# The memory layer of a two-layer trunk: rows read back through DRAM, one transpose for the sample's sums, a low split issued later, a bias on GpSimd, two PSUM pools exchanged

## The chip, the cores and the metric

The kernel runs on one core of one Trainium2 chip. The metric is the device time of one execution in microseconds; 956.14 us is the median of three runs of the kernel before.

Engines are named as the profile names them: PE (TensorE matmul, with its weight load PEld), DVE (VectorE), ACT (ScalarE), POOL (GpSimd), SP (SyncE, which issues the DMAs).

## The reference

One inference step of a two-layer trunk with 256 prompt tokens and 8 samples of 8 tokens, width 1024. Layer 0 mixes tokens by a gated spatial MLP, layer 1 by an mLSTM matrix memory of 8 heads (keys 128 wide, values 256 wide); a gated MLP with a short convolution follows each. The change lies in the memory layer, whose core is, for each head and chunk:

```python
qk, new_buf = causal_dwconv(qk_pre, conv_buf, conv_w, conv_b)
qk = silu(qk)                                   # q, and k scaled
...
w_intra = jnp.exp(D - m_t[..., None])           # gates, masked
w_inter = jnp.exp(inter - m_t)
sc = einsum('bhtd,bhsd->bhts', qc, kc) * w_intra
num = w_inter * einsum('bhtd,bhde->bhte', qc, C) + einsum('bhts,bhse->bhte', sc, vc)
den = w_inter * einsum('bhtd,bhd->bht', qc, n) + sum(sc)
h = num / maximum(abs(den), exp(-m_t))
...
C_new = decay * C + einsum('bhsd,bhse->bhde', kg, vc)
...
hn = (h - mean(h)) * rsqrt(var(h) + EPS) * gn_g
y = (sigmoid(o_pre) * hn) @ w_out
```

Prompt and samples share the weights, so all 320 tokens go through each projection together, and the samples' memories C are eight inputs and eight outputs per head.

## The kernel before

**Projections.** All weights come from DRAM in the order in which they are used, as pieces of up to 128 x 1024 (`raw`, four buffers, issued by SP four pieces ahead). Each is split for precision into a high part `wh` (a cast on ACT, line 154) and a low part `wl` (a subtraction on DVE, line 155), three buffers each, made one piece ahead. `chunk` then issues 24 matmuls for the 8 k-steps of a piece: `wh` with the high part of the activations, `wh` with their low part, `wl` with the high part. `block` does one output block of 128 x 320 and accumulates it in a bank of the PSUM pool `psm` (three banks, tag `pm`). All else uses the pool `psa` (five banks, tag `pa`). Banks of a pool are given out in turn, so an operation that takes a bank waits for the last reader of what stood in it.

**Order.** The order on PE is the order of the program. The splits are pinned in the program's order too (`hold`). The other instructions of DVE, ACT, POOL and SP are placed by a list scheduler that knows the data dependences and has a cost for each; `issue_after` puts an instruction behind a given one, and `pin` fixes its place among its neighbours.

**Memory layer** (`layer_b`; some 420 to 716 us of the span). `gates` computes the rows of all heads' gates, 8 x 392 (`Xf`), and their two-part form `X`. A loop over the heads h then does, in this order: the projections of `q` and `k`, with convolution and SiLU (`qk_epi`: POOL copies, ACT `bcv` line 765, DVE `bcv` line 767); the attention of head h-1 with its states (`inter`, `numer`), its statistics (`stats`: DVE `t`, POOL `sl` line 953, DVE `nb` line 957, ACT `hn` line 965); the two blocks of `v` (`v_epi`, copied by ACT to `vTb`, lines 785 and 786); the scores (`scores`); the two blocks of the output gate (`o_epi`: DVE `o_b` line 995, ACT `th_o`); `finish` of head h-1 (transposes `phn`, DVE `y_b` line 1009, ACT `yhb`, DVE `ylb` line 1012); the state updates of the samples (`state_sample`: PE `pcs`, DVE `C` line 990, and the store `out_Cs`); and the natural forms of k and v (`k_nat`, `v_nat`: transposes `pk` and `pv`).

- The rows reach all 128 partitions in `scores` by a matmul, `pMb`, with a selector `sel` of 128 x 8 x 128. ACT's `w` (line 805) and DVE's `qw` and `dec` read its bank.
- The normalised sums `hn` are [128, 3, 256]: two thirds for the prompt, the last third for the 64 rows of the samples, padded with zeros. Six 128 x 128 transposes bring them back, three for each half of 256, and each half has its own `y_b` of 320 columns.
- In `o_epi(h, 1, blk())` the gate's second block takes a weight piece and so issues the split of the next one; `finish(h - 1)` follows.
- `early` runs blocks of the output projection ahead, in the heads 5 to 7 (two of them at the end of the head of number 4): they read `yhb`, `ylb` of the heads done.
- Head 7 has no next head: its second gate block comes after `pCp` (`state_prompt`) in the tail, then the rest of the output projection.

Of the kernel before, what the change touches and what calls it, by code (L numbers as in the profile page):

```python
# [37 lines left out]
class Net:  # L38
# [26 lines left out]
    def weights(self):  # L65
# [48 lines left out]
        self.loaded, self.halved, self.used = [], [], 0  # L114

# [4 lines left out]
    def prefetch(self, n, m):  # L120
# [8 lines left out]
        while len(self.halved) < min(m, len(self.wq)):  # L129
# [25 lines left out]
            self.last_low = nc.vector.tensor_tensor(wl[:, :kn, :], raw[:, :kn, :], wh[:, :kn, :].bitcast(F32), op=SUB)  # L155
            self.hold(self.last_low)
            self.halved.append((wh, wl))

# [26 lines left out]
    def block(self, kt, rhs):  # L185

        ps = self.psm.tile([P, 512], F32, tag="pm", name="pm")
# [447 lines left out]
    def layer_b(self):  # L635
# [5 lines left out]
        with ExitStack() as ctx:  # L641
# [6 lines left out]
            sel = lp.tile([P, NH, P], F32R, name="sel")  # L648
# [12 lines left out]
            def gates(rp):  # L661
# [3 lines left out]
                selr = rp.tile([P, NH, P], F32, name="selr")  # L665
# [59 lines left out]
                nc.scalar.activation(Xf[:, T:392], wi, AF.Exp)  # L725
                nc.vector.tensor_copy(X[0:8], Xf)
# [61 lines left out]

            def scores(h):
# [3 lines left out]
                pb = self.psa.tile([P, 512], F32, tag="pa", name="pMb")  # L793
                sc = self.psa.tile([P, 512], F32, tag="pa", name="psc")
                if h:
                    mm(pb[:, :392], sel[:, h, :], X, True, True)
# [3 lines left out]
                if not h:  # L800

                    mm(pb[:, :392], sel[:, h, :], X, True, True)
# [11 lines left out]
                dec = hp.tile([P, NB], F32, tag="dec", name="dec", bufs=2)  # L814
                nc.vector.tensor_copy(dec, pb[:, 384:392])
# [39 lines left out]
            def k_nat(h):  # L855
                s = S[h]
                ks = s["k"][0]
                pk = self.psa.tile([P, 512], F32, tag="pa", name="pk")
# [72 lines left out]
            def stats(h, between=None):  # L931
# [19 lines left out]
                self.t_made = nc.vector.scalar_tensor_tensor(t1, t1, 1e-36, mv[:, :, 1], op0=MAX, op1=ADD)  # L951
                sl = hp.tile([P, 3], F32, tag="sl", name="sl", bufs=1)
                nc.gpsimd.tensor_tensor(sl, t1, self.mhalf.to_broadcast([P, 3]), op=ALU.pow)
                if between:
                    between()
                nb = hp.tile([P, 3], F32, tag="nb", name="nb", bufs=1)
                made = nc.vector.scalar_tensor_tensor(nb, mv[:, :, 0], -1.0, sl, op0=MULT, op1=MULT)
                if between:
                    self.pin(made)
                for t in range(3):  # L960
# [39 lines left out]
            def finish(h):  # L1000
# [3 lines left out]
                for e in range(2):  # L1004
                    pt = self.psa.tile([P, 512], F32, tag="pa", name="phn")
                    for t in range(3):
                        self.tr(pt[:, t * P:(t + 1) * P], hn[:, t, e * P:(e + 1) * P], self.ident)
# [292 lines left out]
```

## Time and profile before

| | |
|---|---|
| median of 3 runs | 956.14 us (955.89 to 956.53) |
| profiled execution | 956.05 us |
| its span | 954.3 us |
| PE clock granted in it | 0.999 |
| busy: PE, PEld, DVE, ACT, POOL | 947.3, 933.8, 697.3, 531.9, 115.8 us |
| DMA | 155.19 MB, 163 GB/s mean |

The profile is one execution on the chip. A row of a timeline gives start, duration (of all instructions in the row, where it ends in x2 and more), engine, line and operation, output and inputs, and in brackets the idle time before it with what ended it. Matmuls are pipelined, so a matmul's cost is read from start to start. A row of stretches gives start:end, the length, and then PE, PEld, DVE, ACT and POOL busy time with instruction counts, the PE clock, the share of the DMA engines and GB/s.

### The profile page before, as it was taken

To read this page: it belongs to the slowest core of one execution; us is meant where nothing else is said; L and a number is where in the kernel's file an instruction comes from. 1 tells how busy PE (TensorE), PEld (TensorE's weight loads), DVE (VectorE), ACT (ScalarE), POOL (GpSimd) and SP (SyncE) were. 2 spreads that over 40 slices of the span, in tenths; PEclk is the share of its full clock that TensorE was granted. 3 is DMA by queue.
4 is the path that set the end of the run, shared out by engine and by line. 5 is a ranking of instruction groups with operands and counts; after the bars stand their busy time and mean duration, and the time that the engine had idled before them with its cause. 6 is when DMAs were issued, how large, how long until landed. Compare 5 with 4: busy or idle time off the path is not lost.

```text
span 954.3 us, 17131 instructions
## 1 busy us (share of the span) xinstructions
PE 947.3 (99%) x6427; PEld 933.8 (98%) x6427; DVE 697.3 (73%) x1331; ACT 531.9 (56%) x978; POOL 115.8 (12%) x291
## 2 busy tenths in 40 slices
PE   9999999999999999999999999999999999999997
PEld 8889999999999999999999999999999999999997
DVE  6766976577777754559999998788897777775443
ACT  7557543454555443458777876666766445544342
POOL 2200000010000000014333322102102000000000
PEclk9999999999999999999999999999999999999999
DMA  8643346444444465565465655553474444445441
GB/s 270 210 153 133 133 137 198 160 146 147 149 156 155 139 183 147 149 216 175 128 212 175 206 178 196 185 183 118 132 247 148 149 145 154 156 144 155 143 141 56
DMA packets 54214, 155.19 MB, mean 163 GB/s; under 512 B 7372, under 2 KB 11980, under 8 KB 54132
## 3 DMA queue, kind: packets, MB, share of 16 engines
q1 hardware_dynamic: 54132, 154.10, 50.5%
q8 instruction: 51, 0.84, 0.4%
q14 instruction: 31, 0.25, 0.1%
HBM read 142.10 MB, written 11.97 MB: 161 GB/s over the span
## 4 chain that ended last, share of the span: by engine, by line
PE 94%; DVE 3%; ACT 1%; POOL 1%; DMA 0%; issue 0%; SPq 0%; POOLq 0%
PE pm L54 81%; PE pv_a L54 6%; PE num L54 2%; PE pmix L54 1%; PE pcs L54 1%; PE psc L54 1%; PE phn L57 0%; PE pCp L54 0%; DMA raw<-in_a_wv 0%; PE pv L57 0%; DVE wl L155 0%; PE pc L54 0%; DVE bcv L767 0%; PE pg L54 0%; PE pk L57 0%
## 5 line engine op out<-in xcount | busy, mean ns | idle before, releaser
L154 ACT CAST wh<-raw 128x1024 fp32r<-128x1024 f32 (+3 forms) x256 | 257.0, 1004 | 294.1 <-PE pm L54 161.7
L155 DVE TENSOR_TENSOR wl<-raw,wh 128x1024 fp32r<-128x1024 f32 (+3 forms) x256 | 299.0, 1169 | 118.9 <-ACT wh L154 115.0
L54 PE MATMUL pm<-xh,wh 128*128 128x320 f32 x1216 | 372.3, 311 | 0.1
L54 PE MATMUL pm<-xl,wh 128*128 128x320 f32 x1216 | 370.3, 309 | 0.0
L54 PE MATMUL pm<-xh,wl 128*128 128x320 f32 x1216 | 321.2, 309 | 0.0
L54 PEld LDWEIGHTS pm<-xh,wh 128*128 128x128 f32 x1216 | 228.4, 188 | 0.4 <-DVE o_b L995 0.3
L54 PEld LDWEIGHTS pm<-xl,wh 128*128 128x128 f32 x1216 | 228.4, 188 | 0.2
L54 PEld LDWEIGHTS pm<-xh,wl 128*128 128x128 f32 x1216 | 214.5, 188 | 0.0
L54 PE MATMUL pm<-yh_f,wh 128*128 128x320 f32 x352 | 108.8, 309 | 0.0
L54 PE MATMUL pm<-yl_f,wh 128*128 128x320 f32 x352 | 108.8, 309 | 0.0
L54 PE MATMUL pm<-yh_f,wl 128*128 128x320 f32 x352 | 108.8, 309 | 0.0
L54 PEld LDWEIGHTS pm<-yh_f,wh 128*128 128x128 f32 x352 | 66.1, 188 | 0.0
L54 PEld LDWEIGHTS pm<-yl_f,wh 128*128 128x128 f32 x352 | 66.1, 188 | 0.0
L54 PEld LDWEIGHTS pm<-yh_f,wl 128*128 128x128 f32 x352 | 66.1, 188 | 0.0
L531 DVE SCALAR_TENSOR_TENSOR fcv<-fpad,vecs,fcv 128x336 f32<-128x336 f32 x88 | 49.6, 565 | 2.1 <-ACT fcv L529 0.7
L54 PE MATMUL pm<-yh_a,wh 128*128 128x320 f32 x128 | 39.6, 310 | 0.0
L54 PE MATMUL pm<-yh_a,wl 128*128 128x320 f32 x128 | 39.5, 309 | 0.0
L54 PE MATMUL pm<-yl_a,wh 128*128 128x320 f32 x128 | 39.5, 309 | 0.0
L533 ACT ACTIVATE fgl<-fcv 128x256 f32<-128x256 f32 x44 | 18.2, 414 | 37.8 <-DVE fcv L531 37.8
L54 PE MATMUL pm<-yhb,wh 128*128 128x320 f32 x128 | 38.1, 311 | 0.0
L54 PE MATMUL pm<-ylb,wh 128*128 128x320 f32 x128 | 37.8, 309 | 0.0
L303 DVE TENSOR_TENSOR xT<-pm,xT 128x320 f32<-128x320 f32 x39 | 19.1, 489 | 25.1 <-PE pm L54 24.9
(286 smaller groups left out, 1371.7 us busy)
## 6 DMA issues: line engine op xcount, KB each, us to landing
raw<-in_f_up SPq DMA_DIRECT2D x88, 512.0 KB, 3.3
raw<-in_b_win SPq DMA_DIRECT2D x48, 512.0 KB, 4.0
raw<-in_f_dn SPq DMA_DIRECT2D x32, 448.0 KB, 3.3
C<-in_C SPq DMA_DIRECT2D x32, 258.0 KB, 3.7
out_Cs<-C SPq DMA_DIRECT2D x32, 258.0 KB, 2.5
raw<-in_a_win SPq DMA_DIRECT2D x16, 512.0 KB, 3.3
raw<-in_a_wo SPq DMA_DIRECT2D x16, 512.0 KB, 4.3
raw<-in_f_dn SPq DMA_DIRECT2D x16, 512.0 KB, 3.5
```

The costliest lines, as they stand in the source:

```text
L54: self.pin(self.nc.tensor.matmul(out, lhsT, rhs, start=start, stop=stop, skip_group_check=skip))
L154: self.last_split = self.hold(nc.scalar.copy(wh[:, :kn, :], raw[:, :kn, :]))
L155: self.last_low = nc.vector.tensor_tensor(wl[:, :kn, :], raw[:, :kn, :], wh[:, :kn, :].bitcast(F32), op=SUB)
L303: self.nc.vector.tensor_tensor(x, ps[:, :T], x, op=ADD)
L531: nc.vector.scalar_tensor_tensor(cv, pd[:, i:i + NC], self.vec(w + i * KF), cv, op0=MULT, op1=ADD)
L533: nc.scalar.activation(gl[:, :TP], cv[:, :TP], AF.Gelu_apprx_tanh)
```

## The change

- `gates` writes the rows `Xf` to a DRAM buffer; for h of 1 and more `rows_in(h)` reads row h back into all partitions (`Mb`, two buffers), and `scores` uses it in place of the `pMb` matmul. Head 0 keeps the matmul. `sel` shrinks to 128 x 128, and `dec` is copied for head 0 alone.
- The samples' normalised sums go to `hs` [128, 128], the two halves of 128 one above the other; one transpose brings them back. `y_b` becomes two instructions over both halves, one for the prompt (2 x 256) and one for the samples (2 x 64).
- For heads 1 to 6 the low split issued by the gate's second block is put off and issued behind the first `y_b` of `finish`.
- `nb` is computed on POOL from a negated mean `nm` (DVE).
- `pk` of `k_nat` takes a bank of `psm` (h < 7); head 7's second gate block takes one of `psa`; a further `prefetch` stands behind `begin(2)`.

The order of matmuls and transposes on PE stays as it was, but for the 7 `pMb` and 8 `phn` that are gone. On the other engines the scheduler makes a new order: on DVE `o_b`, `y_b` (2 x 256), `wl`, `y_b` (2 x 64), two `C`, `kgs`, two `ylb`; on ACT the three `w` of the next head stand before its `bcv`, at the end of the head before; on SP the read of `Mb` stands right behind the store `out_Cs` of the fourth state step, and `rows` is written after `out_m`.

```diff
@@ -112,6 +112,7 @@
         ffn(1)
         self.wq = q
         self.loaded, self.halved, self.used = [], [], 0
+        self.late, self.put_off = [], False
 
     AHEAD, SPLIT_AHEAD = 4, 1
     low_last = False
@@ -152,9 +153,16 @@
                 self.halved.append((wh, wl))
                 continue
             self.last_split = self.hold(nc.scalar.copy(wh[:, :kn, :], raw[:, :kn, :]))
-            self.last_low = nc.vector.tensor_tensor(wl[:, :kn, :], raw[:, :kn, :], wh[:, :kn, :].bitcast(F32), op=SUB)
-            self.hold(self.last_low)
             self.halved.append((wh, wl))
+            self.late.append((wl[:, :kn, :], raw[:, :kn, :], wh[:, :kn, :]))
+            if not self.put_off:
+                self.low_parts()
+
+    def low_parts(self):
+
+        for wl, raw, wh in self.late:
+            self.last_low = self.hold(self.nc.vector.tensor_tensor(wl, raw, wh.bitcast(F32), op=SUB))
+        self.late = []
 
     @contextmanager
     def behind_split(self):
@@ -182,9 +190,10 @@
                 if sweep:
                     self.mm(ps[:, :T], wl[:, k, :], xh, False, last and k == kn - 1)
 
-    def block(self, kt, rhs):
-
-        ps = self.psm.tile([P, 512], F32, tag="pm", name="pm")
+    def block(self, kt, rhs, ps=None):
+
+        if ps is None:
+            ps = self.psm.tile([P, 512], F32, tag="pm", name="pm")
         done = 0
         while done < kt:
             kn = self.wq[self.used][3]
@@ -645,7 +654,7 @@
             gnh = lp.tile([P, 16], F32, name="gnh")
             colsT = lp.tile([P, 3, 96], F32, name="cols")
             X = lp.tile([P, 392], F32R, name="X")
-            sel = lp.tile([P, NH, P], F32R, name="sel")
+            sel = lp.tile([P, P], F32R, name="sel")
             mk = lp.tile([P, NB], F32, name="mk")
             mo = lp.tile([8, 9], F32, name="mo")
             pads = []
@@ -662,7 +671,7 @@
 
                 bif = rp.tile([40, 1 + NB], F32, name="bif")
                 rst = rp.tile([40, 2, T], F32, name="rst")
-                selr = rp.tile([P, NH, P], F32, name="selr")
+                selr = rp.tile([P, P], F32, name="selr")
                 RS = rp.tile([P, 384], F32, name="RS")
                 nc.sync.dma_start(bif, I["b_if"])
                 nc.sync.dma_start(rst, I["seg"])
@@ -723,6 +732,8 @@
                 nc.vector.tensor_tensor(seg(wi[:, :64]), m0.unsqueeze(2).to_broadcast([8, NB, NS]), seg(M[:, TP:]), op=SUB)
                 nc.vector.tensor_tensor(wi[:, 64:72], m0, ML, op=SUB)
                 nc.scalar.activation(Xf[:, T:392], wi, AF.Exp)
+
+                nc.sync.dma_start(I["rows"], Xf)
                 nc.vector.tensor_copy(X[0:8], Xf)
                 nc.vector.tensor_tensor(X[32:40], Xf, X[0:8].bitcast(F32), op=SUB)
                 nc.vector.tensor_scalar(gnh, self.vecs[:, V_GN:V_GN + 16], 0.5, None, op0=MULT)
@@ -786,20 +797,23 @@
                 nc.scalar.copy(vT[:, T:384], ps[:, TP:T])
                 S[h].setdefault("vT", []).append(vT)
 
+            def rows_in(h):
+                mb = hp.tile([P, 392], F32, tag="Mb", name="Mb", bufs=2)
+                nc.sync.dma_start(mb, I["rows"][h:h + 1, :].to_broadcast([P, 392]))
+                S[h]["rows"] = mb
+
             def scores(h):
                 s = S[h]
                 q, qh, ql = s["q"]
                 k, kh, kl = s["k"]
-                pb = self.psa.tile([P, 512], F32, tag="pa", name="pMb")
+                pb = s["rows"] if h else self.psa.tile([P, 512], F32, tag="pa", name="pMb")
                 sc = self.psa.tile([P, 512], F32, tag="pa", name="psc")
-                if h:
-                    mm(pb[:, :392], sel[:, h, :], X, True, True)
                 mm3(sc[:, :TP], kh, kl, qh, ql, True, True)
                 mm(sc[:, TP:384], k[:, P:TP], q[:, P:TP], True, True)
                 mm(sc[:, 384:448], k[:, TP:384], q[:, TP:T], True, True)
                 if not h:
 
-                    mm(pb[:, :392], sel[:, h, :], X, True, True)
+                    mm(pb[:, :392], sel, X, True, True)
                 w = hp.tile([P, 448], F32, tag="w", name="w", bufs=1)
                 for (n, o, c0, c1, t) in ((P, 0, 0, TP, 0), (P, TP, P, TP, 1), (64, 384, TP, T, 2)):
                     nc.scalar.activation(w[:n, o:o + c1 - c0], pb[:n, c0:c1], AF.Exp, scale=-1.0, bias=colsT[:n, t, h:h + 1])
@@ -811,8 +825,10 @@
                                         channel_multiplier=1)
                 nc.gpsimd.affine_select(w3, w3, pattern=[[NS, NB], [1, NS]], compare_op=ALU.is_ge, fill=0.0, base=0,
                                         channel_multiplier=-1)
-                dec = hp.tile([P, NB], F32, tag="dec", name="dec", bufs=2)
-                nc.vector.tensor_copy(dec, pb[:, 384:392])
+                dec = pb[:, 384:392]
+                if not h:
+                    dec = hp.tile([P, NB], F32, name="dec")
+                    nc.vector.tensor_copy(dec, pb[:, 384:392])
                 qw = hp.tile([P, 64], F32, tag="qw", name="qw", bufs=1)
                 nc.vector.scalar_tensor_tensor(qw, q[:, TP:T], 0.5, pb[:, T:384], op0=MULT, op1=MULT)
                 Qd = Qz.rearrange("p (b e) -> p b e", e=136)
@@ -855,7 +871,8 @@
             def k_nat(h):
                 s = S[h]
                 ks = s["k"][0]
-                pk = self.psa.tile([P, 512], F32, tag="pa", name="pk")
+                pool, tag = (self.psm, "pm") if h < NH - 1 else (self.psa, "pa")
+                pk = pool.tile([P, 512], F32, tag=tag, name="pk")
                 for t in range(3):
                     self.tr(pk[:, t * P:(t + 1) * P], ks[:, t * P:(t + 1) * P], self.ident)
                 kgh = hp.tile([P, 2, P], F32R, tag="kgh", name="kgh", bufs=1)
@@ -949,20 +966,27 @@
                 t1 = hp.tile([P, 3], F32, tag="t1", name="t1", bufs=1)
                 nc.vector.scalar_tensor_tensor(t1, rd, EPS, rd, op0=MULT, op1=MULT)
                 self.t_made = nc.vector.scalar_tensor_tensor(t1, t1, 1e-36, mv[:, :, 1], op0=MAX, op1=ADD)
+                nm = hp.tile([P, 3], F32, tag="nm", name="nm", bufs=1)
+                nc.vector.tensor_scalar(nm, mv[:, :, 0], -1.0, None, op0=MULT)
                 sl = hp.tile([P, 3], F32, tag="sl", name="sl", bufs=1)
                 nc.gpsimd.tensor_tensor(sl, t1, self.mhalf.to_broadcast([P, 3]), op=ALU.pow)
+                nb = hp.tile([P, 3], F32, tag="nb", name="nb", bufs=1)
+                nc.gpsimd.tensor_tensor(nb, nm, sl, op=MULT)
                 if between:
                     between()
-                nb = hp.tile([P, 3], F32, tag="nb", name="nb", bufs=1)
-                made = nc.vector.scalar_tensor_tensor(nb, mv[:, :, 0], -1.0, sl, op0=MULT, op1=MULT)
-                if between:
-                    self.pin(made)
-                for t in range(3):
-                    n = P if t < 2 else 64
-                    if h == NH - 1 and t:
-                        nc.vector.tensor_scalar(hn[:n, t, :], src[t][:n, :DV], mv[:n, t, 0:1], sl[:n, t:t + 1], op0=SUB, op1=MULT)
+                last = h == NH - 1
+                for t in range(2):
+                    if last and t:
+                        nc.vector.tensor_scalar(hn[:, t, :], src[t][:, :DV], mv[:, t, 0:1], sl[:, t:t + 1], op0=SUB, op1=MULT)
                     else:
-                        nc.scalar.activation(hn[:n, t, :], src[t][:n, :DV], AF.Identity, scale=sl[:n, t:t + 1], bias=nb[:n, t:t + 1])
+                        nc.scalar.activation(hn[:, t, :], src[t][:, :DV], AF.Identity, scale=sl[:, t:t + 1], bias=nb[:, t:t + 1])
+
+                for e in range(2):
+                    a, z = hs[64 * e:64 * e + 64, :], ns[:, e * P:(e + 1) * P]
+                    if last:
+                        nc.vector.tensor_scalar(a, z, mv[:64, 2, 0:1], sl[:64, 2:3], op0=SUB, op1=MULT)
+                    else:
+                        nc.scalar.activation(a, z, AF.Identity, scale=sl[:64, 2:3], bias=nb[:64, 2:3])
 
             def state_prompt(h):
                 s = S[h]
@@ -993,20 +1017,29 @@
             def o_epi(h, j, ps):
                 o = lp.tile([P, T], F32, tag="ob", name="o_b", bufs=1)
                 nc.vector.tensor_tensor(o, ps[:, :T], self.rb, op=MULT)
-                th = lp.tile([P, T], F32, tag="tho", name="th_o", bufs=4)
-                nc.scalar.activation(th, o, AF.Tanh, scale=0.5)
-                S[h].setdefault("o", []).append(th)
+                if not j:
+                    S[h]["o"] = lp.tile([P, 2, T], F32, tag="tho", name="th_o", bufs=2)
+                nc.scalar.activation(S[h]["o"][:, j, :], o, AF.Tanh, scale=0.5)
 
             def finish(h):
                 s = S[h]
                 yh = hp.tile([P, 2, T], F32R, tag="yhb", name="yhb", bufs=6)
                 yl = hp.tile([P, 2, T], F32R, tag="ylb", name="ylb", bufs=6)
+                pt, ps = [self.psa.tile([P, 512], F32, tag="pa", name="phn") for _ in range(2)]
                 for e in range(2):
-                    pt = self.psa.tile([P, 512], F32, tag="pa", name="phn")
-                    for t in range(3):
-                        self.tr(pt[:, t * P:(t + 1) * P], hn[:, t, e * P:(e + 1) * P], self.ident)
-                    y = self.tp.tile([P, T], F32, tag="yf", name="y_b", bufs=2)
-                    nc.vector.scalar_tensor_tensor(y, s["o"][e], 1.0, pt[:, :T], op0=ADD, op1=MULT)
+                    for t in range(2):
+                        self.tr(pt[:, (2 * e + t) * P:(2 * e + t + 1) * P], hn[:, t, e * P:(e + 1) * P], self.ident)
+                self.tr(ps[:, :P], hs, self.ident)
+                yb = lp.tile([P, 2, T], F32, name="y_b", bufs=1)
+                o = s["o"]
+                for c, n, x in ((slice(0, TP), TP, pt), (slice(TP, T), 64, ps)):
+                    made = nc.vector.scalar_tensor_tensor(yb[:, :, c], o[:, :, c], 1.0, x[:, :2 * n].rearrange("p (e t) -> p e t", e=2), op0=ADD, op1=MULT)
+                    if self.put_off:
+                        self.put_off = False
+                        with tc.issue_after(made.ins):
+                            self.low_parts()
+                for e in range(2):
+                    y = yb[:, e, :]
                     g = gnh[:, 2 * h + e:2 * h + e + 1]
                     nc.scalar.activation(yh[:, e, :], y, AF.Copy, scale=g)
                     nc.vector.scalar_tensor_tensor(yl[:, e, :], y, g, yh[:, e, :].bitcast(F32), op0=MULT, op1=SUB)
@@ -1025,8 +1058,8 @@
             vb = hp.tile([P, CW], F32R, name="vb")
             Qz = hp.tile([P, 8 * 136], F32R, name="Qz")
             Ps = hp.tile([P, P], F32R, name="Ps")
-            hn = hp.tile([P, 3, DV], F32, name="hn")
-            nc.gpsimd.memset(hn[64:, 2, :], 0.0)
+            hn = hp.tile([P, 2, DV], F32, name="hn")
+            hs = hp.tile([P, P], F32, name="hs")
             nc.gpsimd.memset(vh[:, :, DV:DV + 1].bitcast(F32), 1.0)
             nc.gpsimd.memset(vh[:, :, DV + 1:].bitcast(F32), 0.0)
             nc.gpsimd.memset(vl[:, :, DV:].bitcast(F32), 0.0)
@@ -1056,6 +1089,7 @@
 
             for h in range(NH):
                 if h:
+                    rows_in(h)
                     qk_epi(h, 0, blk())
                     early(h, 0)
                     if h == 1:
@@ -1099,8 +1133,8 @@
                     for i in (0, 1):
                         state_split(h, i)
                 if h and not last:
+                    self.put_off = True
                     o_epi(h, 1, blk())
-                if h and not last:
                     finish(h - 1)
                     state_sample(h - 1, 3)
                 k_nat(h)
@@ -1133,10 +1167,11 @@
             v_first(h)
             state_prompt(h)
             k_mask(h)
-            o_epi(h, 1, blk())
+            o_epi(h, 1, self.block(KD, self.x_rhs, self.psa.tile([P, 512], F32, tag="pa", name="pm")))
             finish(h)
             state_sample(h, 0)
             begin(2)
+            self.prefetch(0, self.used + 2)
             state_sample(h, 1)
             for m in range(KD):
                 ps = part.get(m)
...
@@ -1280,6 +1313,7 @@
     arrays = _lay_out({k: np.asarray(v) for k, v in inputs.items()})
     nc = bacc.Bacc("TRN2", target_bir_lowering=False, num_devices=1)
     I = {k: nc.dram_tensor("in_" + k, v.shape, F32, kind="ExternalInput").ap() for k, v in arrays.items()}
+    I["rows"] = nc.dram_tensor("rows", (NH, 392), F32).ap()
     O = {k: nc.dram_tensor("out_" + k, s, F32, kind="ExternalOutput").ap() for k, s in _OUTS.items()}
     with tile.TileContext(nc) as tc:
         Net(nc, tc, I, O).run()
```

More of the change, by code (lines that the diff above doesn't have):

```diff
@@ L1262, in _lay_out @@
     a["seg"] = seg
-    sel = np.zeros((P, NH, P), f)
-    for h in range(NH):
-        sel[h, h] = 1.0
-        sel[32 + h, h] = 1.0
+    sel = np.zeros((P, P), f)
+    sel[[0, 32]] = 1.0
     a["sel"] = sel
```

## The prediction

> **What bounds the kernel now.** I read the page's busy times and its chain of work first, then what TensorE (PE) waited for, the table of stretches, and the timelines of PE, VectorE (DVE), GpSimd (POOL) and ScalarE (ACT) around the edits.
>
> ```profile
> PE 947.3 (99%) x6427; PEld 933.8 (98%) x6427; DVE 697.3 (73%) x1331; ACT 531.9 (56%) x978; POOL 115.8 (12%) x291
> ...
> PE 94%; DVE 3%; ACT 1%; POOL 1%; DMA 0%; issue 0%; SPq 0%; POOLq 0%
> ```
>
> ```profile
> PE pv L57 <- DVE y_b L1009: 0.6, 1, 0.6
> ```
>
> ```profile
> 449.00:479.00 30.00, 29.23 (x210) 28.56 (x208) 28.68 (x73) 23.96 (x59) 10.87 (x24) 1.00 0.50 149
> ```
>
> PE works through the whole span and its clock is 1.00: a microsecond is won only by issuing less on PE or by closing a gap in it. The one named gap in the memory layer is in head 1 (the stretch from 449 us; the columns after the length are PE, weight load, DVE, ACT, POOL). DVE is busy 28.68 of 30 us there, so whatever is moved on DVE moves something else.
>
> **The change part by part**
>
> *Rows read back.* Seven `pMb` matmuls go (heads 1 to 7).
>
> ```profile
> 467.75 0.34 PE L54 MATMUL pMb<-X,sel 128*128 128x392 f32 x1
> 467.93 0.30 PE L54 MATMUL psc<-qh,kh 128*128 128x256 f32 x1
> ```
>
> From its start to the next start is 0.18 us: 7 x 0.18 = 1.26 us of PE issue, with nothing else put there: **-1.26**. The same rows now come by one DMA of 1.5 KB each way; what they may hold up stands in the last rival.
>
> *One transpose for the sample's sums.* Eight heads issue five transposes instead of six.
>
> ```profile
> 505.65 0.82 PE L57 MATMUL phn<-ident,hn 128*128 128x128 f32 x6
> ...
> 506.88 0.82 PE L57 MATMUL pv<-ident,vTb 128*128 128x128 f32 x6
> 507.45 0.36 PE L54 MATMUL num<-Ch,Qz 128*128 128x258 f32 x1
> ```
>
> Six transposes of this form (`pv`, 506.88 to 507.45) take 0.57 us, so one is 0.095, rounded to 0.10: **-0.8**.
>
> *The split behind the gate's step.* The rows of head 1 on PE and on DVE:
>
> ```profile
> 477.26 0.60 PE L57 MATMUL pv<-ident,vTb 128*128 128x128 f32 x4
> 478.44 0.44 PE L57 MATMUL pv<-ident,vTb 128*128 128x128 f32 x2 [0.58 <-DVE y_b L1009]
> 478.93 0.36 PE L54 MATMUL num<-Ch,Qz 128*128 128x258 f32 x1
> ```
>
> ```profile
> 476.37 1.22 DVE L155 TENSOR_TENSOR wl<-raw,wh 128x1024 fp32r<-128x1024 f32 x1
> 477.51 0.48 DVE L995 TENSOR_TENSOR o_b<-pm,rb 128x320 f32<-128x320 f32 x1
> 477.91 0.87 DVE L1009 SCALAR_TENSOR_TENSOR y_b<-th_o,phn 128x320 f32<-128x320 f32 x2
> ```
>
> From the first `pv` to `num` PE needs 1.67 us here and 0.57 in head 2 (506.88 to 507.45): 1.10 us of waiting for the bank that `y_b` reads, because a low split of 1.14 us (476.37 to 477.51) was put ahead of `o_b`. In the new order the DVE runs `o_b`, the first `y_b`, then the split. What is late next? `num` now needs the bank of that first `y_b`, of 2 x 256. Head 2 gives the start:
>
> ```profile
> 505.92 0.49 DVE L995 TENSOR_TENSOR o_b<-pm,rb 128x320 f32<-128x320 f32 x1 [0.47 <-PE pm L54]
> ```
>
> ```profile
> 472.71 0.56 DVE L824 SCALAR_TENSOR_TENSOR Pf<-psc,w 128x384 f32<-128x384 f32 x1 [0.23 <-POOL w L807]
> ```
>
> `o_b` starts 0.27 after the first transpose (505.65 to 505.92), `y_b` 0.40 later (477.51 to 477.91). The new `y_b` has 512 columns: at least the 0.56 of a 384-column one, at most the 0.87 of the pair; I take 0.65, since it is one instruction. It ends 1.32 after the first transpose (1.23 to 1.54), and `num` is due at 1.80 less one transpose, 1.70. So no wait in any of heads 1 to 6, and the whole **-1.1** is gained.
>
> *The last gate block in the other pool.*
>
> ```profile
> 683.77 0.28 PE L54 MATMUL pCp<-vl,kgh 128*128 128x258 f32 x1
> 683.89 0.28 PE L54 MATMUL pCp<-vh,kgl 128*128 128x258 f32 x1
> 684.22 0.42 PE L54 MATMUL pm<-xh,wh 128*128 128x320 f32 x1
> ```
>
> 0.33 us from the last `pCp` to the gate block, where the `pCp` before it was followed after 0.12: **-0.2**, as it no longer waits for the previous gate's `o_b` to free its bank. `k_nat` in the small pool costs nothing: the bank that its turn there brings was last read by the state update that DVE runs ahead of `o_b`, and `o_b` is done 0.27 + 0.49 us after the first transpose (head 2's rows), `pk` comes after all five.
>
> *What the later split makes late.* The early blocks of the output projection (after heads 4, 5, 6) use both `ylb` and low parts that DVE now makes after the split.
>
> ```profile
> 564.59 1.18 DVE L1012 SCALAR_TENSOR_TENSOR ylb<-y_b,gnh,yhb 128x320 fp32r<-128x320 f32 x2
> ...
> 566.20 0.34 DVE L870 SCALAR_TENSOR_TENSOR kgs<-pk,cols,kgs 32x128 fp32r<-32x128 f32 x1
> ...
> 569.90 2.35 DVE L155 TENSOR_TENSOR wl<-raw,wh 128x1024 fp32r<-128x1024 f32 x2
> ```
>
> ```profile
> 562.72 0.82 PE L57 MATMUL phn<-ident,hn 128*128 128x128 f32 x6
> ...
> 567.28 0.31 PE L54 MATMUL pm<-ylb,wh 128*128 128x320 f32 x1
> ...
> 570.95 1.34 PE L54 MATMUL pm<-yhb,wl 128*128 128x320 f32 x8
> ```
>
> With head 2's steps the new DVE order runs, counted from the first transpose: `o_b` at 0.27, the first `y_b` at 0.67, the split at 1.32 (1.14 long), the second `y_b` (0.15), two state updates (0.4 each, the step from `o_b` to `y_b`), `kgs` (0.34, with its neighbour's overlap 0.3): `ylb` starts at 3.7 and ends at 4.9. Head 4's transposes began at 562.72, so the matmul of 567.28 is due at 4.56, 0.1 earlier without the sixth transpose: **+0.4** (0 to 0.6). The low part read at 570.95, due at 8.2 - 0.1 + 0.4 = 8.5, is now the split behind all that: from `kgs` to the split DVE took 3.70 us (566.20 to 569.90), of which that `kgs` and a residual add, 0.8, fall away; 3.7 + 1.1 for the two `ylb` + 2.9 + 1.2 for the split is 8.9: **+0.4** (0.1 to 0.7). After heads 5 and 6, where more blocks lie between, I put **+0.15** for both.
>
> ```profile
> 695.66 1.22 DVE L155 TENSOR_TENSOR wl<-raw,wh 128x1024 fp32r<-128x1024 f32 x1
> ```
>
> ```profile
> 697.10 1.34 PE L54 MATMUL pm<-yhb,wl 128*128 128x320 f32 x8
> ```
>
> Behind head 7 the low part ends at 696.88, only 0.22 before its matmul. The extra prefetch and the earlier gate block change what stands in front of such a split on DVE by one step of 0.4 to 0.9 (a state update or a residual add): **+0.4** (0 to 0.6).
>
> *Bias by GpSimd.* `nb` leaves DVE, where it waited for POOL's `sl`, and follows it on POOL:
>
> ```profile
> 468.09 0.86 POOL L953 TENSOR_TENSOR sl<-t,mhalf 128x3 f32<-128x3 f32 x1 [0.82 <-DVE t L951]
> ...
> 495.61 1.77 POOL L953 TENSOR_TENSOR sl<-t,mhalf 128x3 f32<-128x3 f32 x1 [2.27 <-DVE t L951]
> ```
>
> ```profile
> 495.45 1.21 DVE L155 TENSOR_TENSOR wl<-raw,wh 128x1024 fp32r<-128x1024 f32 x1
> 497.41 0.16 DVE L957 SCALAR_TENSOR_TENSOR nb<-mv,sl 128x3 f32<-128x3 f32 x1 [0.75 <-POOL sl L953]
> ```
>
> ```profile
> 470.89 0.21 ACT L786 COPY vTb<-pm 128x64 f32<-128x64 f32 x1
> ...
> 499.32 0.21 ACT L786 COPY vTb<-pm 128x64 f32<-128x64 f32 x1
> ```
>
> ```profile
> 472.51 0.31 PE L54 MATMUL pm<-xh,wh 128*128 128x320 f32 x1
> ...
> 502.13 0.31 PE L54 MATMUL pm<-xh,wh 128*128 128x320 f32 x1
> ```
>
> DVE stops standing idle for 0.75 us in head 2, and only a non-critical engine gains by that. Behind `nb` queue the normalisation and the copies `vTb` on ACT, whose end frees the bank of the second gate block: 1.4 us of slack in head 1 (471.10 to 472.51), 2.6 in head 2 (499.53 to 502.13). `nb` on POOL lies between 0.2 us (as `nb` on DVE) and another 1.77; I take 0.5, covered by that slack: **0**.
>
> The sum: -1.26 - 0.8 - 1.1 - 0.2 + 0.4 + 0.4 + 0.15 + 0.4 = **-2.0 us**. The profiled execution took 956.05 us (a span of 954.3 and 1.75 around it), 0.09 below the median of the runs, 956.14. So 954.1 us against the median. About 0.2%, 1.9 us, is what a measurement can tell from no change.
>
> **The Trainium skill on the bias.** Where DVE sits in a two-input split (495.45), `sl` took 1.77 us, where that was not beside it (468.09) 0.86. The Trainium skill, GPSIMD Engine Reference, section "Engine selection", says to keep elementwise arithmetic on VectorE, and section "Specifications" that GpSimd's interfaces to SBUF are shared with VectorE, in contention when it runs with two SBUF inputs. The two rows agree with that, and it speaks against this part. Its price is the second rival.
>
> **The rivals**
>
> *1. The late splits do not bite* (the new waits of 1.35 us are absent): -3.36 us, 952.8 us. For it: each of the four is smaller than one DVE step, and PE needs nothing else new. Against: DVE is the fuller engine here.
>
> *2. The bias is slow.* Both POOL steps stand beside splits, 2 x 1.77 us. In head 1 they end at 468.09 + 3.54 = 471.63 instead of 469.1, 2.5 later, against 1.4 of slack: +1.1. In head 2 they end at 499.15 instead of 497.57, 1.6 later, inside 2.6. Sum -0.9 us: 955.2. Or the late parts cost their upper ends (0.6, 0.7, 0.3, 0.6 instead of 1.35 in all): -1.15, 955.0. Both are no change.
>
> *3. Slower: the rows land late.* The `w` exponentials no longer follow a matmul but a DMA, and stand on ACT at the end of the head before, with casts `wh` and the `bcv` steps of the next `q` queued behind them; on SP the read stands behind the state's store and ahead of weights.
>
> ```profile
> 508.62 0.47 DVE L990 SCALAR_TENSOR_TENSOR C<-C,dec,pcs 128x258 f32<-128x258 f32 x1
> ```
>
> ```profile
> 513.33 0.67 ACT L765 ACTIVATE bcv<-bpad,vecs 128x344 f32<-128x344 f32 x1
> ```
>
> ```profile
> raw<-in_b_win SPq DMA_DIRECT2D x48, 512.0 KB, 4.0
> ...
> out_Cs<-C SPq DMA_DIRECT2D x32, 258.0 KB, 2.5
> ```
>
> The buffer of the rows is free when the state update at 508.62 ends (509.1). At 2.5 to 4.0 us to landing the rows are there at 511.6 to 513.1, ahead of `bcv` at 513.33, and ACT goes on. It decides from a landing of about 6 us: then `bcv`, the conversions behind it and the scores of heads 2 to 7 come 2 us or more later, and their margin is some 2.5. At +0.7 in each of six heads, +4.2 - 2.0 = +2.2: 958.3 us. For it: DMA engines are half busy here (0.50 in the stretch), and it hits every head. Against: no row above lands that late.
>
> **How the numbers follow.** Forecast (953.3 to 954.9, its four waits up or down by half) 0.40; rival 1 0.20; rival 2 in its two forms 0.21; rival 3 0.19. The forecast's own interval straddles the 0.2% bound (954.2): a bit over half of it (0.23), with rival 1 and a little of rival 2 (0.03), gives faster 0.46; the rest of both (0.17 and 0.18) same 0.35; the third rival slower 0.19. The range goes from rival 1 with nothing to spare (952.3) up to four fifths of the third rival's price (957.4), and leaves out about 2 in 10.
>
> **What would show it.** Right: no `pMb` after head 0, five `phn` per head, no wait of PE for `y_b` at head 1, short waits of PE for `ylb` or `wl` after head 4 and behind head 7. Wrong: PE waiting for `psc` operands, or for a copy of `vTb`, in several heads; `w` waiting for a DMA on ACT for microseconds; `sl` with `nb` above 3 us in head 1.

## The result, and the profile after

The changed kernel took 967.50 us (median of 4 runs, 967.42 to 968.83) against 956.03 us before: ratio 1.0122 (95% interval 1.0105 to 1.014), 11.5 us slower. The forecast was 954.1 us, with a range up to 957.4.

The page's busy times and chain of the kernel after:

```profile
PE 947.5 (98%) x6412; PEld 931.9 (97%) x6412; DVE 700.7 (73%) x1325; ACT 535.6 (55%) x985; POOL 123.5 (13%) x298
...
PE 86%; DVE 9%; ACT 2%; issue 1%; DMA 1%; POOL 1%; SPq 0%; DVEq 0%; ACTq 0%
```

What PE waited for, after (total, times, longest):

```profile
PE pm L54 <- DVE wl L164: 7.7, 7, 1.5
PE pcs L54 <- ACT vTb L797: 2.1, 1, 2.1
PE pm L54 <- DVE ylb L1045: 1.0, 2, 0.7
...
PE num L54 <- DVE y_b L1036: 0.8, 3, 0.3
```

The stretch of head 1, after (columns as in the prediction):

```profile
449.00:479.00 30.00, 27.89 (x199) 27.64 (x200) 25.32 (x67) 24.01 (x60) 13.12 (x23) 1.00 0.46 150
```

PE issues 15 instructions fewer and its clock is the same, but 8% of the chain has gone from PE to others. DVE has hardly more work than before (700.7 us against 697.3): it comes late with nearly the same work. In the stretch of head 1 it is even less busy, 25.32 us against 28.68. The gap that the change aimed at (`pv` waiting for `y_b`) is gone, and other waits have come: for low parts `wl` behind the gate step of each of heads 1 to 6 (after heads 1 to 3 in the next head's block of `k`, after heads 4 to 6 in an output block) and once in the tail, for `vTb` in head 1, for `ylb` after head 4, and small ones for `y_b`.

Head 2 on PE and DVE, after (its transposes start at 507.57):

```profile
507.57 0.60 PE L57 MATMUL phn<-ident,hn 128*128 128x128 f32 x4
...
509.86 0.36 PE L54 MATMUL num<-Ch,Qz 128*128 128x258 f32 x1 [0.34 <-DVE y_b L1036]
...
518.24 1.43 PE L54 MATMUL pm<-xh,wl 128*128 128x320 f32 x8 [1.34 <-DVE wl L164]
```

```profile
507.43 1.29 DVE L919 TENSOR_TENSOR Cl<-C,Ch 128x516 fp32r<-128x516 f32 x2
508.64 0.48 DVE L1019 TENSOR_TENSOR o_b<-pm,rb 128x320 f32<-128x320 f32 x1
509.04 0.68 DVE L1036 SCALAR_TENSOR_TENSOR y_b<-th_o,phn 128x512 f32<-128x512 f32 x1
509.63 1.22 DVE L164 TENSOR_TENSOR wl<-raw,wh 128x1024 fp32r<-128x1024 f32 x1
...
512.24 1.90 DVE L1045 SCALAR_TENSOR_TENSOR ylb<-y_b,gnh,yhb 128x320 fp32r<-128x320 f32 x2
...
516.97 1.21 DVE L164 TENSOR_TENSOR wl<-raw,wh 128x1024 fp32r<-128x1024 f32 x1
```

The split put off (509.63) is that of the next piece, for `q`. The low part that PE lacks at 518.24 is the one after it, for `k`, made at 516.97, at the end of all that stands behind the gate. Each split is matched to its block by counting the splits and the blocks in the order of the pieces. Before, the split for the same block of `k` stood ahead of `o_b`:

```profile
504.24 1.22 DVE L155 TENSOR_TENSOR wl<-raw,wh 128x1024 fp32r<-128x1024 f32 x1
```

It ended 8.9 us before PE read it at 514.34; after, PE resumes 0.06 us after it ends. A word on the description above: it says that `hold` pins the splits. In the memory layer it does not; it pins them only at the start of the first layer, so here the scheduler moves every split, and each edit moves others.

### The profile page after: what moved, and what is told of

Same layout as the page of the kernel before. It is cut to its first block, busy times and chain, and to the rows that moved or that the text cites. A ratio compares the mean times of both kernels' runs of the same rounds, so it can differ in the third digit from the quotient of the medians.

```text
span 965.6 us, 17092 instructions
## 1 busy us (share of the span) xinstructions
PE 947.5 (98%) x6412; PEld 931.9 (97%) x6412; DVE 700.7 (73%) x1325; ACT 535.6 (55%) x985; POOL 123.5 (13%) x298
## 4 chain that ended last, share of the span: by engine, by line
PE 86%; DVE 9%; ACT 2%; issue 1%; DMA 1%; POOL 1%; SPq 0%; DVEq 0%; ACTq 0%
PE pm L54 74%; PE pv_a L54 6%; PE num L54 2%; DVE wl L164 2%; DVE Cl L919 1%; DVE C L1014 1%; PE pmix L54 1%; DVE ylb L1045 1%; DMA out_Cs<-C 1%; DVE vl L862 1%; POOL sl L972 1%; PE pCp L54 1%; DVE y_b L1036 1%; DVE kgs L887 0%; DVE o_b L1019 0%
```

## The experiments

Each run is compared with runs of the kernel before on the same chip (medians of 955.97 to 956.22 us). Lines of the diffs are cut to what differs.

### The parts taken back out of the change

No put-off:

```diff
-                    self.put_off = True
```

> The changed kernel with the split not put off; every other edit stays. Theory A (the put-off split sets the order: the low part of the piece after it, which the kernel before made ahead of the gate step, now comes at the end of the DVE queue behind it): the six waits of PE for wl in the heads 1 to 6 (1.35, 1.50, 1.48, 0.67, 1.66, 1.66, together 8.3 us) go, so about 959 us, with the wait of head 1 for vTb left. Theory B (the other parts made DVE and POOL late and the split only shows it): the waits move to another operand and the time falls by less than 3 us, to 965 or more.

Measured: 970.62 us, ratio 1.0153 (1.0138 to 1.0168): slower still. PE's waits:

```profile
PE num L54 <- DVE y_b L1036: 8.0, 6, 2.1
PE pcs L54 <- ACT vTb L797: 3.7, 2, 2.1
...
PE pm L54 <- DVE wl L164: 0.3, 1, 0.3
```

The waits for `wl` of heads 1 to 6 do go, as theory A says, but others as large come for `y_b`, with a split in front of it on DVE (head 2):

```profile
510.78 1.21 DVE L164 TENSOR_TENSOR wl<-raw,wh 128x1024 fp32r<-128x1024 f32 x1
511.92 0.87 DVE L1036 SCALAR_TENSOR_TENSOR y_b<-th_o,phn 128x512 f32<-128x512 f32 x2
```

These waits add up to 12.0 us, those of the change (`wl`, `vTb`, `ylb`, `y_b`) to 11.6, which does not explain 3 us more. The clock does, in the profiled execution: PE worked twice for 3.4 us at half its clock, which no other profile shows in the memory layer.

```profile
474.89:478.31 3.42, 3.42 (x15) 3.42 (x14) 3.15 (x6) 3.17 (x9) 1.19 (x3) 0.50 0.26 73
546.57:549.98 3.41, 3.41 (x15) 3.41 (x14) 3.25 (x9) 1.80 (x5) 2.04 (x2) 0.50 0.81 263
```

```profile
477.29 0.47 PE L54 MATMUL pm<-xh,wh 128*128 128x320 f32 x1
477.55 0.47 PE L54 MATMUL pm<-xl,wh 128*128 128x320 f32 x1
```

A matmul of `pm` takes 0.27 us from start to start there, against 0.15 at full clock: some 13 of them lose 1.5 us in each stretch, about 3 us in all. The mean clock of this kernel's four executions is 0.995 to 0.997, that of the change's four 0.998 to 0.999. Both stretches begin within 1.4 us of the end of a wait of PE of over 2 us (2.1 before 474.23, 2.1 before 545.19), but another wait as long, before 577.70, is followed by none, so why the clock fell stays open. By the waits, then, the put-off neither gains nor loses inside the whole change, and theory A as I had put it, that the put-off is the loss, falls: without it other waits of the same size stand in its place.

Bias back on DVE, with the put-off and without:

```diff
-                nm = ...; nc.vector.tensor_scalar(nm, mv[:, :, 0], -1.0, None, op0=MULT)
-                nc.gpsimd.tensor_tensor(nb, nm, sl, op=MULT)
+                made = nc.vector.scalar_tensor_tensor(nb, mv[:, :, 0], -1.0, sl, op0=MULT, op1=MULT)
+                if between:
+                    self.pin(made)
```

> The changed kernel with the bias back on DVE (nm gone, nb pinned behind sl as before). Theory C (the wait of DVE for sl kept DVE quiet while POOL worked; without it DVE runs two-input steps over it, and sl took 3.25 us in head 1 instead of 0.86): sl falls below 1.8 us in head 1 and the 2.3 us wait of PE for vTb goes, about 965 us. Theory D (sl is long because of what the new rows brought on POOL or DVE, whoever computes nb): sl stays at 3 us and the time at 967.5.

> The changed kernel with both taken back: rows read back, one transpose and the pools are left. By theories A and C together 967.5 - 8.3 - 2.3 = 956.9, less the late ylb and y_b waits (up to 2.6): 954.3 to 957. If A or C is wrong: 960 or more.

Measured: 963.58 us (1.0077, 1.0062 to 1.0092) and 962.32 us (1.0064, 1.0049 to 1.0079). The bias costs 3.9 us in the change (8.3 without the put-off, some 3 of them the clock). As theory C says, PE's wait for `vTb` goes, and `sl` of head 1 falls from 3.25 to 1.90 us, not quite to the 1.8 expected. Without the bias and without the put-off 6 us of loss are left, in rows, transposes and pools, which none of my theories had.

### The parts alone, on the kernel before

Each has the lines of its part from the diff of the change; the put-off stands behind the first of the two old `y_b`.

> The kernel before with the put-off alone. Theory A: the gap of head 1 goes (-1.1) and the waits for wl come in every one of heads 1 to 6, 6 to 8 us together: 961 to 963 us. Theory B: the put-off alone gains its 1.1 us and costs little: 955 us.

> The kernel before with the rows read back and nothing else. Theory E (the w exponentials, free of the matmul, are ordered at the end of the head before, where they wait for the read of Mb and hold ACT, then bcv on DVE, then the gate step): ACT waits for Mb for 5 us or more in all, PE waits for y_b in most of heads 1 to 6, and the time is 959 to 962 us in spite of the 1.26 us of matmuls that go. Theory F (the rows cost nothing; the loss without put-off and bias comes from the new y_b and its banks): 955 us.

> The kernel before with the samples' sums in one transpose and y_b in 2 x 256 and 2 x 64, nothing else. Theory E: gains its 0.8 us, and num waits for the first y_b instead of the second, so 954.5 to 956 us. Theory F: num waits for y_b in heads 1 to 6, 959 us or more.

> The kernel before with pk in the small pool, the last gate block in the large one and the further prefetch, nothing else. Both theories: -0.2 us for the last gate block, up to +0.5 for the low part in the tail: 955.8 to 956.5 us. If pk's new bank makes PE wait, or psa with one user less lets num start earlier, it shows as a change of over 1 us.

> The kernel before with the bias on GpSimd, nothing else. Theory C (DVE no longer stops for sl, runs two-input steps over it and stretches it): sl goes to 1.8 us or more in more heads than the four of before, and head 1, with 1.4 us of slack, loses up to 2: 956.5 to 959 us. If only the rows' early steps make sl long, it stays as it was: 955.8 to 956.2 us.

| part alone | us | ratio (95% interval) |
|---|---|---|
| put-off | 963.81 | 1.0079 (1.0062 to 1.0096) |
| rows read back | 956.38 | 1.0006 (0.9996 to 1.0016) |
| one transpose, new `y_b` | 963.54 | 1.0084 (1.0069 to 1.0099) |
| pools, prefetch | 955.20 | 0.9992 (0.9982 to 1.0001) |
| bias on GpSimd | 961.25 | 1.0054 (1.0039 to 1.0069) |

Put-off alone: PE waits for `y_b`, not for `wl`:

```profile
PE num L54 <- DVE y_b L1017: 7.5, 6, 1.3
```

In the old form there are two `y_b`, the split goes between them, and `num` needs the second. The split of `k` is pushed back too (it starts at 513.58 in head 2 and has 1.5 us to spare), but is in time. So nothing of the price comes by theory A's step here: all of it is a split in front of the second `y_b`.

Rows alone: the matmuls go and the time stays. ACT does wait for the read, a few times:

```profile
ACT w L810 <- DMA Mb<-rows: 3.8, 3, 1.4
```

and PE gets waits for `o_b`, `Cl` and `C` (0.6, 0.5 and 0.3 us) that eat the 1.26 us. Theory E has the mechanism and not the size, as the third rival of the prediction did; the time is nearer to theory F's.

Transposes alone: each of heads 1 to 6 waits for `y_b`, as theory F says, and the DVE rows of head 2 show why:

```profile
PE pv L57 <- DVE y_b L1019: 6.4, 6, 2.3
```

```profile
506.98 0.49 DVE L1002 TENSOR_TENSOR o_b<-pm,rb 128x320 f32<-128x320 f32 x1 [0.50 <-PE pm L54]
507.39 1.21 DVE L155 TENSOR_TENSOR wl<-raw,wh 128x1024 fp32r<-128x1024 f32 x1
508.52 0.88 DVE L1019 SCALAR_TENSOR_TENSOR y_b<-th_o,phn 128x512 f32<-128x512 f32 x2
```

The scheduler now puts a split between `o_b` and `y_b`. Counted in the order of the pieces it belongs to the first block of `v`, whose low part PE reads 13.5 us later.

Pools alone: in head 1 `pv` no longer waits; in place of 0.6 us for `y_b`, PE waits 0.4 us there, by the profile for `th_o`. The time is 0.6 us below the lower end of what was expected.

Bias alone: PE waits for `y_b` in heads 1 to 4; the reason stands below, under theory C.

```profile
PE pv L57 <- DVE y_b L1009: 3.3, 4, 0.8
```

### Which split stands in front of the gate (theory G)

From here on a split is held behind the first `y_b` again, but that of the first block of `v`, two pieces behind the next one (`q`):

```diff
+            self.since += 1                 # splits issued since the gate's first y_b
+            if self.gate is not None and self.since == 2:
+                with self.tc.issue_after(self.gate.ins):
+                    self.last_low = ... # the low part
```

> The kernel before with the one transpose and the two new y_b, and one split held behind the first y_b: not the next piece's (q), as in the change, but the one two pieces on (the first block of v), which the scheduler had put between o_b and y_b in the run of the transposes alone and which PE read 13.5 us later. Theory G (the transposes' 7.5 us are that one split of 1.1 us in front of y_b, six times): the waits of PE for y_b go and no wait for wl comes, 954 to 956 us. If the new y_b are late for another reason (their size, their banks): 959 us or more.

> The same with the two pool exchanges and the prefetch. Theory G: 0.8 us less than the run before it, 953.5 to 955 us, under the kernel before. Otherwise 958 or more.

> The same with the rows read back too: everything of the change but the bias on GpSimd, and with the split of v in place of the split of q put off. Theory G: no wait for wl or y_b in heads 1 to 6; the rows add their -1.3 of matmuls and the two or three waits that they had alone (C, Cl, o_b; 1.7 us), 953.5 to 956. If the put-off of q was not what made k's low part late, the waits for wl stay and it is 960 or more.

Measured: 957.15 us (transposes; 1.0013, 1.0003 to 1.0022), 956.34 us (and pools; 1.0004, 0.9994 to 1.0013) and 955.34 us (and rows; 0.9996, 0.9987 to 1.0006). PE's waits for `y_b` in the first and in the third:

```profile
PE pv L57 <- DVE y_b L1024: 1.1, 1, 1.1
```

```profile
PE num L54 <- DVE y_b L1033: 0.8, 2, 0.5
```

Theory G holds: holding one split of each head behind `y_b` takes 6.4 of the transposes' 7.5 us away. The first two times lie 1.2 and 1.3 us above what it had expected, with a wait for `y_b` of 1.1 and 0.9 us left in head 1. Three kernels now differ in the put-off alone, with rows, transposes, pools, and the bias on DVE: nothing put off 962.32, `q` put off 963.58, `v` put off 955.34. The waits for `wl` with `q` and with `v` put off:

```profile
PE pm L54 <- DVE wl L164: 7.1, 7, 1.6
```

```profile
PE pm L54 <- DVE wl L161: 0.3, 1, 0.3
```

So theory A's step is what holding `q`'s split costs. The last kernel, everything of the change but the bias, and with the right split held, can't be told from the kernel before.

### The bias, and what keeps `sl` short (theory C)

The bias on GpSimd, and on DVE one more instruction that waits for `sl` where `nb` stood:

```diff
+                seen = hp.tile([P, 3], F32, tag="seen", name="seen", bufs=1)
+                made = nc.vector.scalar_tensor_tensor(seen, mv[:, :, 0], -1.0, sl, op0=MULT, op1=MULT)
+                if between:
+                    self.pin(made)
```

(`between` is given in head 7 alone, so in the other heads the instruction is not pinned.)

> The kernel before with the bias on GpSimd, and on DVE one small instruction more (128 x 3, its result not used) that waits for sl in the place where nb stood. Theory C (DVE's wait for sl is what kept sl short and the splits behind the casts in step): sl is 0.85 or 1.77 us again, 956 to 957 us. If nb on POOL is itself the cost: 960 us or more as in the run with the bias alone.

Measured: 956.66 us (1.0005, 0.9996 to 1.0015), against 961.25 without that instruction. Added work on DVE that nobody reads gains 4.6 us. POOL rows of head 2, bias alone, then with the instruction:

```profile
496.99 2.98 POOL L955 TENSOR_TENSOR sl<-t,mhalf 128x3 f32<-128x3 f32 x1 [2.33 <-DVE t L951]
500.05 0.19 POOL L957 TENSOR_TENSOR nb<-nm,sl 128x3 f32<-128x3 f32 x1
```

```profile
496.32 1.77 POOL L955 TENSOR_TENSOR sl<-t,mhalf 128x3 f32<-128x3 f32 x1 [2.33 <-DVE t L951]
498.17 0.20 POOL L957 TENSOR_TENSOR nb<-nm,sl 128x3 f32<-128x3 f32 x1
```

In head 2 `nb` itself takes 0.19 us. What costs is that DVE no longer stops: it goes on into `Cl` while POOL works, and `sl` waits (DVE, bias alone):

```profile
497.97 1.28 DVE L902 TENSOR_TENSOR Cl<-C,Ch 128x516 fp32r<-128x516 f32 x2
```

ACT then stands at `hn`, its casts come late, and DVE stands at a split whose cast is not there, with the gate step behind it (bias alone; 2.2 us before, 3.8 with the instruction):

```profile
DVE wl L155 <- ACT wh L154: 14.7, 9, 2.7
```

`sl` grows in heads 2 to 4 alone, not in more heads than before, which theory C had expected, and the time is above its range. In head 1 it is `nb` that waits, beside a `wl` and a `Cl`; with the instruction it takes 0.19 us there too:

```profile
468.20 0.86 POOL L955 TENSOR_TENSOR sl<-t,mhalf 128x3 f32<-128x3 f32 x1 [0.81 <-DVE nm L954]
469.14 1.24 POOL L957 TENSOR_TENSOR nb<-nm,sl 128x3 f32<-128x3 f32 x1
```

The same instruction in the full change, and the full change with both faults mended (the instruction, and the put-off of the right split; in head 1 the split after the next piece's):

> The changed kernel, complete, with the small DVE instruction that waits for sl in the place where nb stood. Theory C: the 3.9 us that the bias cost in the full change go, sl in head 1 falls from 3.25 to under 2 us, about 963.6 us, with the waits for wl left. If the bias costs by POOL's own work: 967 us.

> Every part of the change, with the DVE instruction that waits for sl, and with the split put off being the one two pieces on (in head 1 the next but one, whose use is 8 us away) instead of the next piece's. If the two faults are the whole loss: no wait for wl in heads 1 to 6, none for vTb, 954.5 to 956 us. If something remains between the parts: 958 us or more.

Measured: 966.27 us (1.0103, 1.0088 to 1.0119) and 959.40 us (1.0033, 1.0021 to 1.0046). In the full change `sl` of head 1 falls to 1.91 us (with `nb` 0.20), and PE's wait there from 2.1 to 0.8, and the time by 1.2 us, though the two intervals overlap. That is a third of the 3.9 that the bias costs there. In heads 1 to 4 `sl` is now as long as with the bias on DVE (1.91, 1.77, 1.76, 1.76 us against 1.90, 1.77, 1.76, 1.76), and in heads 5 and 6, where it is 0.9 us longer, PE's waits are the same (1.6 in each), so the length of `sl` is not what the other 2.7 us are. The mended kernel is 4 us above the one with the right split held and the bias on DVE (head 1's split apart, they differ in the bias and the added instruction alone), and in its head 2 a split stands in front of the gate step again. This one is that of `k`, which PE reads 8.0 us after it ends:

```profile
506.54 1.21 DVE L161 TENSOR_TENSOR wl<-raw,wh 128x1024 fp32r<-128x1024 f32 x1
507.67 0.47 DVE L1020 TENSOR_TENSOR o_b<-pm,rb 128x320 f32<-128x320 f32 x1
```

Here `sl` is not short either: 1.84 and 1.90 us in heads 2 and 3, beside a `wl`, where it took 0.85 with the bias on DVE. ACT's waits for the read of the rows are alike in the two (5.0 and 5.9 us). So the bias changes the order on DVE beside the length of `sl`. That the remaining 2.7 us are this order is what the rows suggest; no run holds that order fixed, and it stays open.

### The gap of head 1 by itself

The pools as in the change, and in head 1 alone the split that stood before the second `o_b` held behind the second `y_b` (the old form, both `y_b` of 320):

```diff
+                    made = nc.vector.scalar_tensor_tensor(y, s["o"][e], 1.0, pt[:, :T], op0=ADD, op1=MULT)
+                    if self.mark and e == 1:        # h == 1 alone
+                        self.gate, self.since, self.mark = made, 0, False
...
+            if self.gate is not None and self.since == 1:
+                with self.tc.issue_after(self.gate.ins):
+                    self.last_low = ... # the low part
```

> The kernel before with the pools exchanged and, in head 1 alone, the split that stood before o_b held behind the second y_b. If the gap of head 1 is that split's place and nothing else is late next: the gap of 0.6 to 1.0 us goes, 954.4 to 954.8 us, under the kernel before by 0.15% or so. If the split of k is then late for its use: a wait for wl of up to 1 us in its place, 955.2.

Measured: 954.53 us (954.23 to 955.04), ratio 0.9983 (0.9974 to 0.9992): 1.6 us below the kernel before, and 0.7 below the pools alone. PE's waits, all of them:

```profile
PE pw L54 <- PEq L1292: 0.8, 1, 0.8
PE pm L54 <- DVE o_b L1002: 0.2, 1, 0.2
```

The wait of head 1 (0.6 us before, 0.4 with the pools alone) is gone and nothing took its place. How much of the gain is the pools' and how much the split's is not shown closer than by these two runs.

## Why the prediction was wrong, point by point

Two terms failed most: the low part behind the one put off (7.7 us of waits, where 0.95 stood for heads 4 to 6 and 0.4 for the tail) and the bias (put at 0, worth 3.9).

- **Rows, -1.26.** The matmuls went; alone the part gave +0.4 (-0.4 to +1.5 by its interval). What failed is "nothing else put there": freed from the matmul, `w`, `qw` and `Qz` move to other places on ACT and DVE (`qw` of head 2 from 501.40 to 495.55).
- **Transposes, -0.8.** Alone the part is +7.5. I costed the removed PE work and asked when the new `y_b` would end, but took it that DVE would go from `o_b` to `y_b` in 0.40 us as before. Another split came in between, and it was 1.54 (506.98 to 508.52). With it held elsewhere the part gave +1.2. In the change itself the put-off keeps that place free (508.64 to 509.04), so this loss is not among its 11.5 us.
- **Put-off, -1.1 and "no wait in any of heads 1 to 6".** Head 1's gap went. But in head 2 `o_b` began 1.07 us after the first transpose, not 0.27, because two `Cl` stood before it, and `num` waited 0.34 us.
- **What the later split makes late, +0.95 after heads 4 to 6.** The step that failed: I worked out that the low part behind the queue ends 8.9 us after the first transpose where 8.5 was wanted, and applied it to the output blocks alone. After heads 1 to 3 the next head's block of `k` stands in that place with nearly the same timing (in head 2 before, its low part is read 8.7 us after the first transpose). I took it as made ahead, as in the trace of before, when it is the next one behind the one put off. The queue was also costed too short: in head 2 after, it ends 10.6 us after the first transpose, as `o_b` comes 0.8 us later than I took it and the two `ylb` take 1.90 us instead of 1.1. Measured, of the 7.7 us named above: 3.8 after heads 1 to 3, where I had put nothing, and 3.5 after heads 4 to 6 (0.5, 1.5 and 1.5), where I had put 0.55. After head 5:

```profile
619.70 1.00 PE L54 MATMUL pm<-yhb,wl 128*128 128x320 f32 x5 [1.50 <-DVE wl L164]
```

  `ylb` (0.4 predicted, 1.0 measured) was the smaller part.
- **Tail, +0.4, and pools, -0.2.** PE did wait for a low part in the tail, 0.3 us at 705.62, but not for the one that I had named, which now ends 0.5 us before its matmul; the last gate block, 0.12 us behind the last `pCp`, no longer waited. Pools alone: -0.8 (-1.7 to +0.1).
- **Bias, 0.** The second rival named the mechanism and put it at 1.1 us: `sl` and `nb` at 3.54 us in head 1. Measured 3.25 and 0.19, so over the 3 us that I had named as a sign of being wrong, with 2.1 us of PE's wait for `vTb`; the whole part cost 3.9 in the change. I had seen that DVE's idle 0.75 us before `nb` would vanish and called that a gain without effect; it was the time in which POOL could finish.
- **Third rival, rows late.** ACT's wait for the read, after and in the change without the put-off:

```profile
ACT w L819 <- DMA Mb<-rows: 0.5, 1, 0.5
```

```profile
ACT w L819 <- DMA Mb<-rows: 6.5, 5, 2.2
```

  It is real, in another kernel, and not the cause here.

The range begins at 952.3, half a microsecond under rival 1 as it was worked out (952.8), for no reason given; nothing hangs on it.

One chain of runs leads to the change: 955.34 for all but the bias with the right split held, +8.2 for holding `q`'s split instead, +3.9 for the bias, is 967.5. Such a chain closes by its making, and its steps depend on their order: the bias costs 4.1 with the right split held (and the added instruction), 3.9 with that of `q`. The parts alone (+0.4, +7.5, -0.8, +5.2, +7.6) sum to 20 us instead of 11.5. As I read it, most of them put a split in front of the same step, and that is paid once; no run shows this by itself.

## What to carry to other kernels

Where a scheduler places the instructions of an engine that is close to full, cost an edit by the new order, piece by piece: for each long instruction that is free to move, which operand it makes, when that is read, and what short step on the path it may now stand in front of. Before putting one such instruction off, find out which one has the longest time to its use; putting off the next in line puts off all behind it. A wait that looks idle on one engine can be what keeps it from disturbing another.

## What the runs showed of the hardware

`sl`, three columns wide, takes 0.85 us on POOL when it begins beside `C` on DVE. When it begins beside a subtraction, which reads two SBUF tensors, it ends some 0.7 us after the last of those that follow one another: it takes 1.77 us beside one `wl`, 2.98 beside `wl` and two `Cl`, 3.25 in head 1 of the kernel after:

```profile
468.09 3.25 POOL L972 TENSOR_TENSOR sl<-t,mhalf 128x3 f32<-128x3 f32 x1 [2.35 <-DVE t L968]
471.42 0.19 POOL L974 TENSOR_TENSOR nb<-nm,sl 128x3 f32<-128x3 f32 x1
```

```profile
468.06 1.21 DVE L164 TENSOR_TENSOR wl<-raw,wh 128x1024 fp32r<-128x1024 f32 x1
...
469.33 1.29 DVE L919 TENSOR_TENSOR Cl<-C,Ch 128x516 fp32r<-128x516 f32 x2
```

The Trainium skill, GPSIMD Engine Reference, section "Specifications", says that GpSimd shares its SBUF interfaces with VectorE, in contention with instructions that have two SBUF inputs. These rows agree, and they show how large it is: a small GpSimd step does not run slower beside such instructions, it seems to stand still for as long as they follow one another. `C`, which has one large input in PSUM, did not delay the 0.86 us `sl` of head 1 before, which began at 468.09:

```profile
467.93 0.47 DVE L990 SCALAR_TENSOR_TENSOR C<-C,dec,pcs 128x258 f32<-128x258 f32 x1
```

What runs on DVE as the step begins seems to decide. With the bias alone, `sl` of head 5 began beside `C`; a `Cl` came 0.23 us later and did not lengthen it:

```profile
593.43 0.85 POOL L955 TENSOR_TENSOR sl<-t,mhalf 128x3 f32<-128x3 f32 x1 [3.36 <-DVE t L951]
```

```profile
593.66 1.29 DVE L902 TENSOR_TENSOR Cl<-C,Ch 128x516 fp32r<-128x516 f32 x2
```
